# Float32 activations kept until the down stage, and 30 instead of 27 of 44 down groups by the seven-product scheme

## Chip, cores and metric

The kernel runs on one core of one Trainium2 chip. The metric is the device time of one execution in microseconds (us), the median of several runs. TensorE (PE in the profile) multiplies, VectorE (DVE) adds and subtracts elementwise, ScalarE (ACT) casts and copies, SyncE (SP) issues most loads, and GpSimd (POOL) issues some transfers.

## The reference, cut to what matters

One block of a network on 256 tokens of 2048 channels, in float32: three kinds of attention, gates, an output projection, and a feed-forward part with 5632 hidden channels.

```python
h = rms_norm(x, g_mix); proj = h @ w_in           # then three kinds of attention, gated
...
x = x + merged @ w_out
h2 = rms_norm(x, g_ffn)
u = causal_depthwise_conv(h2 @ w_up, conv_w, conv_b)
u_gate, u_val = jnp.split(u, 2, axis=-1)
x = x + (jax.nn.silu(u_gate) * u_val) @ w_down     # (256 x 5632) @ (5632 x 2048)
```

The change is in the last two products, here called the up stage (`h2 @ w_up`) and the down stage (`a @ w_down`, where `a` is the product of silu(u_gate) and u_val).

## The kernel before, in words

**Three passes for one float32 product.** TensorE multiplies a rounded float32 format (`fp32r`). A float32 operand is split into `hi` (its rounded value, cast by ACT) and `lo` (what is left, subtracted by DVE), and `three` issues three passes for one product: activation hi by weight hi (L382), activation lo by weight hi (L383), activation hi by weight lo (L384). The weights are split as they come (`parts`, L376 and L377): a tile of 128 x 1024 or 128 x 512 is cast into one of four `hi` tiles and subtracted into one of four `lo` tiles. A fifth part can only be cast when TensorE is done with the first one's `hi`, and subtracted when it is done with its `lo`. The raw weights land in a ring of six 512 KB tiles, loaded by SP; a tile comes free when its subtraction is done.

**The down stage.** It has two column blocks of 1024 (`nb` 0 and 1), each walked over 22 pairs of 128-channel rows of `w_down`. A pair is one of 44 groups in all, and a string in `d_plans` says in which order and in which way the groups go (`blocked`):

- `e` (`eight`): eight products, 24 passes of 512 columns; two parts of 1024, loaded plainly (1 MiB).
- `s` (`seven`): the same result by seven products, 21 passes; sums of weight blocks and sums of activation blocks take the place of one product. Four parts (three of 1024, one of 512). The sums of the weights were made in earlier stages and stored in a DRAM tile `kept`; what is loaded is 1.75 MiB. The seven products go into four `Y` banks and three of the four `X` banks of PSUM; after the block's last `s`, `gather` (L409 to L419) adds the `Y` banks to the result `xres`.
- `f` (`form`): the next pair's sums of activation blocks are made (`pair_sums`, L391 to L400: four DVE operations to sum, ACT casts, DVE subtractions).

Before, pairs 0 to 10 in block 0 and 0 to 15 in block 1 go by `s`: 27 of 44. The sums of the weights of two of them (pairs 14 and 15 of block 1) are made by GpSimd with transfers that accumulate in DRAM, late in the up stage (`sums_in_hbm`, `last_sums`). In the up stage each finished 128 x 256 product `a` is split at once (`split_to`, L175 cast and L176 subtract) into the tile `aT`; the last four of the 44 go to `a_ends`.

**Order.** The program text gives an order, and a scheduler of the framework then moves instructions on each engine's queue by its own estimates; only instructions marked `in_order` keep their place. Each engine works its queue strictly in that final order, and waits where an instruction's input isn't there. The end of the program is: the last two `e` groups, X banks added to `xres` on DVE (L1388, L1392), output stored by ACT's queue (L1390 to L1395).

The functions that the diff touches:

## Time and profile before

| what | us |
| --- | --- |
| median of 3 runs (1457.41 to 1457.68) | 1457.41 |
| the profiled execution, its device time | 1458.07 |
| its span from first to last instruction | 1456.4 |
| TensorE busy, of the span | 1451.0 (100%) |
| VectorE busy | 1229.0 (84%) |
| ScalarE busy | 857.1 (59%) |
| GpSimd busy | 31.8 (2%) |

The profile gives a start and a duration for each instruction, and for idle time of an engine what ended it. Successive passes of TensorE overlap, so the time that a pass costs is the distance between two starts, not its own duration. VectorE's instructions also overlap slightly. The down stage begins at 1230.9 us on TensorE.

### The profile page before, as it was taken

How to read it: one execution, taken by the hardware profiler on the slowest of the kernel's cores; microseconds unless marked ns; L12 is line 12 of the kernel's file. 1: busy time of each engine (PE TensorE's matmuls, PEld its weight loads, DVE VectorE, ACT ScalarE, POOL GpSimd, SP SyncE). 2: the span in 40 equal slices, each digit the busy share in tenths (PEclk: the TensorE clock that was granted, in tenths of full speed). 3: DMA queues.
4: the chain of work that ended last, by engine and by line, in shares of the span. 5: the costliest groups of instructions: out<-in, count | busy, mean ns of one | idle time of the engine just before them, and what ended most of it. 6: DMA issues, size and time to landing. Idle time of an engine off the chain costs nothing.

```text
span 1456.4 us, 20650 instructions
## 1 busy us (share of the span) xinstructions
PE 1451.0 (100%) x7290; PEld 1228.8 (84%) x7290; DVE 1229.0 (84%) x1824; ACT 857.1 (59%) x1222; POOL 31.8 (2%) x69
## 2 busy tenths in 40 slices
PE   9999999999999999999999999999999999999998
PEld 7888888888888888888888888888888888888887
DVE  5788778776898899998887888888888877999988
ACT  6755445464564555546676656556556566676775
POOL 0000011010000000000000000000000010000000
PEclk9999999999999999999999999999999999999999
DMA  8797899777668576788877888888888899789996
GB/s 288 223 355 252 308 341 327 267 246 220 213 205 267 181 227 199 270 262 264 303 218 233 289 271 303 281 271 300 282 280 296 275 258 258 247 286 340 326 338 233
DMA packets 169414, 393.41 MB, mean 270 GB/s; under 512 B 12906, under 2 KB 30206, under 8 KB 165086
## 3 DMA queue, kind: packets, MB, share of 16 engines
q1 hardware_dynamic: 165822, 384.87, 79.3%
q0 software_dynamic: 2160, 5.12, 2.0%
q10 hardware_dynamic: 1328, 2.11, 0.4%
q8 instruction: 57, 0.93, 0.3%
q14 instruction: 47, 0.39, 0.1%
HBM read 353.24 MB, written 43.00 MB: 272 GB/s over the span
## 4 chain that ended last, share of the span: by engine, by line
PE 100%; DVE 0%; issue 0%; DVEq 0%
PE u L1315 22%; PE u L1316 11%; PE xg L384 4%; PE xg L383 4%; PE xg L382 4%; PE xd L384 3%; PE xd L383 3%; PE xd L382 3%; PE s L384 2%; PE s L382 2%; PE f L382 2%; PE f L384 2%; PE s L383 2%; PE f L383 2%; PE b L384 2%; PE b L383 2%
## 5 line engine op out<-in xcount | busy, mean ns | idle before, releaser
L1315 PE MATMUL u<-hT,hi_u 128*128 128x512 f32 x1232 | 428.4, 394 | 0.0
L1316 PE MATMUL u<-hT,lo_u 128*128 128x256 f32 x1232 | 341.3, 277 | 0.0
L1315 PEld LDWEIGHTS u<-hT,hi_u 128*128 128x128 f32 x1232 | 231.0, 188 | 53.5
L142 DVE TENSOR_TENSOR lo_u<-raw_u,hi_u 128x1024 fp32r<-128x1024 f32 x176 | 215.1, 1222 | 72.2 <-ACT hi_u L141 71.7
L141 ACT CAST hi_u<-raw_u 128x1024 fp32r<-128x1024 f32 x176 | 184.7, 1050 | 133.3 <-PE u L1315 101.3
L1316 PEld LDWEIGHTS u<-hT,lo_u 128*128 128x128 f32 x1232 | 231.3, 188 | 0.0
L377 DVE TENSOR_TENSOR lo_d<-raw_d,hi_d 128x1024 fp32r<-128x1024 f32 x88 | 106.8, 1221 | 12.9 <-ACT hi_d L376 10.7
L376 ACT CAST hi_d<-raw_d 128x1024 fp32r<-128x1024 f32 x88 | 91.9, 1054 | 36.6 <-PE xd L383 12.6
L376 ACT CAST hi_g<-raw_g 128x1024 fp32r<-128x1024 f32 (+1 forms) x80 | 77.1, 972 | 47.6 <-PE xg L383 21.3
L377 DVE TENSOR_TENSOR lo_g<-raw_g,hi_g 128x1024 fp32r<-128x1024 f32 (+1 forms) x80 | 88.7, 1119 | 5.7 <-ACT hi_g L376 5.3
L384 PE MATMUL xg<-lo_g,xT 128*128 128x512 f32 x175 | 68.1, 389 | 0.0
L382 PE MATMUL xg<-hi_g,xT 128*128 128x512 f32 x175 | 68.1, 389 | 0.0
L383 PE MATMUL xg<-hi_g,xT 128*128 128x512 f32 x175 | 68.1, 389 | 0.0
L141 ACT CAST hi_f<-raw_f 128x1024 fp32r<-128x1024 f32 (+1 forms) x40 | 38.6, 967 | 47.1 <-PE f L383 27.5
L1315 PE MATMUL u<-hT_rest,hi_u 128*128 128x512 f32 x176 | 62.0, 394 | 0.0
L141 ACT CAST hi_b<-raw_b 128x1024 fp32r<-128x1024 f32 x32 | 33.7, 1052 | 45.8 <-PE b L383 14.5
L142 DVE TENSOR_TENSOR lo_f<-raw_f,hi_f 128x1024 fp32r<-128x1024 f32 (+1 forms) x40 | 44.4, 1117 | 17.9 <-ACT hi_f L141 17.8
L1265 ACT ACTIVATE y<-u,taps 128x256 f32<-128x256 f32 x88 | 49.5, 595 | 16.8 <-DVE u L1260 16.7
L141 ACT CAST hi_s<-raw_s 128x1024 fp32r<-128x1024 f32 (+1 forms) x40 | 38.2, 961 | 35.7 <-PE s L383 18.8
L142 DVE TENSOR_TENSOR lo_s<-raw_s,hi_s 128x1024 fp32r<-128x1024 f32 (+1 forms) x40 | 44.6, 1123 | 17.1 <-ACT hi_s L141 17.1
L376 ACT CAST hi_t_g<-t_g 128x1024 fp32r<-128x1024 f32 x30 | 31.5, 1051 | 41.4 <-PE xg L383 39.7
L376 ACT CAST hi_t_d<-raw_t_d 128x1024 fp32r<-128x1024 f32 (+1 forms) x54 | 43.5, 836 | 18.9 <-PE xd L383 11.7
(554 smaller groups left out, 3548.8 us busy)
## 6 DMA issues: line engine op xcount, KB each, us to landing
raw_u<-in_w_up_dram SPq DMA_DIRECT2D x176, 512.0 KB, 4.9
raw_g<-in_w_in_dram SPq DMA_DIRECT2D x96, 512.0 KB, 4.5
raw_d<-in_w_down_dram SPq DMA_DIRECT2D x61, 512.0 KB, 5.8
pre_d<-in_w_down_dram SPq DMA_DIRECT2D x17, 1024.0 KB, 7.6
kept_d<-pre_d SPq DMA_DIRECT2D x17, 1024.0 KB, 6.9
raw_f<-in_w_in_dram SPq DMA_DIRECT2D x32, 512.0 KB, 5.7
raw_s<-in_w_in_dram SPq DMA_DIRECT2D x32, 512.0 KB, 5.7
raw_t_d<-kept_d SPq DMA_DIRECT2D x27, 512.0 KB, 6.1
```

Source lines behind the costliest of these rows:

```text
L141: pin(nc.scalar.copy(hi[:, :m], raw[:, :m]))
L142: pin(nc.vector.tensor_tensor(lo[:, :m], raw[:, :m], hi[:, :m].bitcast(F32), ALU.subtract))
L376: nc.scalar.copy(hi[:, :n], src)
L377: nc.vector.tensor_tensor(lo[:, :n], src, hi[:, :n].bitcast(F32), ALU.subtract)
L382: fix(nc.tensor.matmul(o, lhsT=ah, rhs=w[0], start=first, stop=False))
L383: fix(nc.tensor.matmul(o, lhsT=al, rhs=w[0], start=False, stop=False))
L384: fix(nc.tensor.matmul(o, lhsT=ah, rhs=w[1], start=False, stop=last))
L1265: nc.scalar.activation(y, u[:, 2:], AF.Identity, scale=tap(2), bias=tap(3))
L1315: nc.tensor.matmul(ps[i], lhsT=hi[:, j, c], rhs=hT(k + j), start=first, stop=False)
L1316: nc.tensor.matmul(ps[i][:, :S], lhsT=lo[:, j, c], rhs=hT(k + j)[:, :S], start=False, stop=last)
```

## The change

**Groups.** The plans are new. `t` is a `seven` whose weight sums are not loaded: its two plain tiles are loaded, and four DVE additions of 128 x 512 make the sums (`made`). Block 0 has 8 `e` and 14 sevens (two of them `t`: pairs 4 and 9); block 1 has 6 `e` and 16 sevens (three `t`: pairs 6, 10 and 13), in the order of pairs 5 to 15, then 0 to 4. The GpSimd sums are gone. 25 groups have their weight sums made ahead, in both versions.

**Activations.** For pairs 0 to 13 the up stage writes the float32 product and the three block sums into one tile `a_raw` of eight 128 x 128 blocks (`raw_sums`), and splits nothing. In the down stage an `f` of block 0 splits seven of these blocks at once (`split_raw`: one ACT cast and one DVE subtraction of 128 x 896); `lo` goes where the previous pair's raw tile was, `hi` into one of nine slots. Pairs 9 to 13 overwrite the slots of 0 to 4, so `hi` of 0 to 4 is stored to DRAM (448 KB each, ACT's queue) and loaded again in block 1 (`back`, SP's queue). Only pairs 14 and 15 still have `pair_sums` in the down stage.

```diff
-        "efefefef" + "sef" * 4 + "ssefsfssfssee",
-        "efsss" * 3 + "efssfsssssee",
+        "efefeffef" + "sfsfsfs" + "eftfss" + "fsfs" + "etfsfs" + "ss" + "ee",
+        "estse" + "fsfste" + "fssfte" + "fsfsfss" + "sss" + "ee",
...
+        def made(p):
+            raw0, raw1 = load(2 * p), load(2 * p + 1)
+            raw2 = raw_tile(f"raw_t_{name}{nb}_{p}")
+            raw3 = t4_tile(f"raw_t4_{name}{nb}_{p}")
+            nc.vector.tensor_tensor(raw2[:, :512], raw0[:, :512], raw0[:, 512:], ALU.add)
+            nc.vector.tensor_tensor(raw0[:, 512:], raw0[:, 512:], raw1[:, 512:], ALU.add)
+            nc.vector.tensor_tensor(raw2[:, 512:], raw2[:, :512], raw1[:, 512:], ALU.add)
+            nc.vector.tensor_tensor(raw3, raw2[:, 512:], raw1[:, :512], ALU.add)
+            return raw0, raw1, raw2, raw3
...
+    def raw_sums(p):
+        v = raw_blocks(p).rearrange("p (i q) -> p i q", i=8)
+        a01 = v[:, 7:8].to_broadcast([P, 2, P])
+        nc.vector.tensor_tensor(v[:, 2:4], v[:, 5:7], a01, ALU.subtract)
+        nc.vector.scalar_tensor_tensor(v[:, 0], v[:, 2], -1.0, v[:, 6], ALU.mult, ALU.subtract)
+        nc.vector.tensor_tensor(v[:, 1], v[:, 0], v[:, 4], ALU.add)
...
+            if p < n_raw:
+                c = 768 - 256 * j
+                nc.vector.tensor_tensor(raw_blocks(p)[:, c : c + S], g, y, ALU.mult)
+                if j:
+                    raw_sums(p)
+                return
             nc.vector.tensor_tensor(g, g, y, ALU.mult)
-            a_done.append(a_pair(f // 2)[:, f % 2])
-            split_to(a_done[-1], g)
+            split_to(a_pair(p)[:, j], g)
...
+    def split_raw(p):
...
+        hi = place_at(p % n_at)
+        place_of[p] = hi, lo
+        nc.scalar.copy(hi, w[:, : 7 * P])
+        nc.vector.tensor_tensor(lo, w[:, : 7 * P], hi.bitcast(F32), ALU.subtract)
+        if p < moved:
+            left[p] = dram.tile([P, 7 * P], F32, tag=f"left_{p}", name=f"left_{p}")
+            nc.scalar.dma_start(left[p], hi.bitcast(F32))
+
+    def back(p):
+        hi = place_at((moved + p) % n_at)
+        place_of[p] = hi, place_of[p][1]
+        nc.sync.dma_start(hi.bitcast(F32), left[p])
```

In the up stage and before it, TensorE's order is the same in both. In the down stage the order moves, and three places of it matter below. The rows give the line, the operation, and output and inputs by the program's names; line 360 of the changed kernel is line 377 of the one before (subtract into `lo`), and 365, 366 and 367 are 382, 383 and 384 (the three passes).

First, VectorE ahead of the first weight part of pair 4 of block 0 (tiles `d0_8`, `d0_9`), which is the first `t`. Before, the subtractions of parts stand among the sums for the activations (`fw`):

```order
L391 TENSOR_TENSOR fw_7_12345<-aT_6752 128x512
L377 TENSOR_TENSOR lo_d0_36_12312<-raw_d0_36_12309,hi_d0_36_12311 128x1024
L394 TENSOR_TENSOR fw_7_12345<-fw_7_12345 128x256
L377 TENSOR_TENSOR lo_d0_37_12330<-raw_d0_37_12327,hi_d0_37_12329 128x1024
L395 SCALAR_TENSOR_TENSOR fw_7_12345<-fw_7_12345 128x128
L400 TENSOR_TENSOR aT_6752<-fw_7_12345,aT_6752 128x128
L396 TENSOR_TENSOR fw_7_12345<-fw_7_12345 128x128
L377 TENSOR_TENSOR lo_d0_8_12364<-raw_d0_8_12354,hi_d0_8_12363 128x1024
L400 TENSOR_TENSOR sf_11752<-fw_7_12345,sf_11752 128x3x128
L377 TENSOR_TENSOR lo_d0_9_12374<-raw_d0_9_12357,hi_d0_9_12373 128x1024
```

VectorE at the same place of the changed kernel, where line 1375 is the split of a pair's activations and lines 463 to 466 are the four additions of the `t`:

```order
L360 TENSOR_TENSOR lo_d0_36_12153<-raw_d0_36_12150,hi_d0_36_12152 128x1024
L360 TENSOR_TENSOR lo_d0_37_12171<-raw_d0_37_12168,hi_d0_37_12170 128x1024
L1375 TENSOR_TENSOR a_lo8_12186<-a_raw8_9060,sf_more_12187 128x896
L463 TENSOR_TENSOR raw_t_d0_4_12194<-raw_d0_8_12190 128x512
L1375 TENSOR_TENSOR a_lo9_12237<-a_raw9_9104,sf_11730 128x896
L464 TENSOR_TENSOR raw_d0_8_12190<-raw_d0_8_12190,raw_d0_9_12192 128x512
L465 TENSOR_TENSOR raw_t_d0_4_12194<-raw_t_d0_4_12194,raw_d0_9_12192 128x512
L1375 TENSOR_TENSOR a_lo10_12332<-a_raw10_9514,sf_11730 128x896
L466 TENSOR_TENSOR raw_t4_d0_4_12195<-raw_t_d0_4_12194,raw_d0_9_12192 128x512
L360 TENSOR_TENSOR lo_d0_8_12201<-raw_d0_8_12190,hi_d0_8_12200 128x1024
```

Three splits and four additions now stand between the subtraction of the preceding `e` group (`d0_37`) and that of the `t` group's first part.

Second, TensorE at that group. Before, a part's three passes follow each other, with its `lo` third:

```order
L382 MATMUL yd0_0_11986<-hi_d0_8_12363,aT_6752 128x512
L383 MATMUL yd0_0_11986<-hi_d0_8_12363,aT_6752 128x512
L384 MATMUL yd0_0_11986<-lo_d0_8_12364,aT_6752 128x512
L382 MATMUL yd0_3_11989<-hi_d0_8_12363,sf_11752 128x512
L383 MATMUL yd0_3_11989<-hi_d0_8_12363,sf_11752 128x512
L384 MATMUL yd0_3_11989<-lo_d0_8_12364,sf_11752 128x512
```

TensorE in the changed kernel, same group:

```order
L365 MATMUL yd0_0_11953<-hi_d0_8_12200,sf_11730 128x512
L366 MATMUL yd0_0_11953<-hi_d0_8_12200,a_lo4_11948 128x512
L365 MATMUL yd0_3_11956<-hi_d0_8_12200,sf_11730 128x512
L366 MATMUL yd0_3_11956<-hi_d0_8_12200,a_lo4_11948 128x512
L365 MATMUL xd0_0_0_11731<-hi_d0_9_12210,sf_11730 128x512
L366 MATMUL xd0_0_0_11731<-hi_d0_9_12210,a_lo4_11948 128x512
L365 MATMUL xd0_0_1_11732<-hi_d0_9_12210,sf_11730 128x512
L366 MATMUL xd0_0_1_11732<-hi_d0_9_12210,a_lo4_11948 128x512
L365 MATMUL yd0_2_11955<-hi_t_d0_4_12220,sf_11730 128x512
L366 MATMUL yd0_2_11955<-hi_t_d0_4_12220,a_lo4_11948 128x512
L367 MATMUL yd0_0_11953<-lo_d0_8_12201,sf_11730 128x512
L367 MATMUL yd0_3_11956<-lo_d0_8_12201,sf_11730 128x512
```

The first pass that needs `lo` of `d0_8` is now the eleventh of its group and no longer the third. At some other places of the changed down stage the `lo` passes are put back in the same way, by a few passes.

Third, VectorE at the end of the program. Before, the last addition of `gather` (L419) stands behind the first of the four X additions (L1388):

```order
L413 TENSOR_TENSOR xres_again_5681<-xres_again_5681,e_1024_13834 128x512
L415 TENSOR_TENSOR e_1024_13834<-e_1024_13834,yd1_3_12895 128x512
L416 TENSOR_TENSOR xres_again_5681<-xres_again_5681,e_1024_13834 128x512
L418 TENSOR_TENSOR e_1024_13834<-e_1024_13834,yd1_2_12894 128x512
L1388 TENSOR_TENSOR xres_again_5681<-xres_again_5681,xd1_0_0_12839 128x512
L419 TENSOR_TENSOR xres_again_5681<-xres_again_5681,e_1024_13834 128x512
L1388 TENSOR_TENSOR xres_again_5681<-xres_again_5681,xd1_0_1_12840 128x512
L1388 TENSOR_TENSOR xres_again_5681<-xres_again_5681,xd1_1_0_12841 128x512
L1388 TENSOR_TENSOR xres_again_5681<-xres_again_5681,xd1_1_1_12842 128x512
L1392 TENSOR_TENSOR xres_again_5681<-xres_again_5681,apart_13870 128x256
```

VectorE at the end of the changed kernel:

```order
L396 TENSOR_TENSOR xres_again_5681<-xres_again_5681,e_1024_13749 128x512
L398 TENSOR_TENSOR e_1024_13749<-e_1024_13749,yd1_3_12836 128x512
L1432 TENSOR_TENSOR xres_again_5681<-xres_again_5681,xd1_0_0_12793 128x512
L399 TENSOR_TENSOR xres_again_5681<-xres_again_5681,e_1024_13749 128x512
L1432 TENSOR_TENSOR xres_again_5681<-xres_again_5681,xd1_0_1_12794 128x512
L401 TENSOR_TENSOR e_1024_13749<-e_1024_13749,yd1_2_12835 128x512
L1432 TENSOR_TENSOR xres_again_5681<-xres_again_5681,xd1_1_0_12795 128x512
L402 TENSOR_TENSOR xres_again_5681<-xres_again_5681,e_1024_13749 128x512
L1432 TENSOR_TENSOR xres_again_5681<-xres_again_5681,xd1_1_1_12796 128x512
L1436 TENSOR_TENSOR xres_again_5681<-xres_again_5681,apart_13785 128x256
```

The four late additions of `gather` (L398 to L402) are now spread among the X additions (L1432), and the last of them stands between the third and the fourth. Just ahead of the last two `e` groups, in both blocks, the addition of the second Y bank (L393, L410 before) also moved: before, it stood behind the subtractions of the first two parts of the `ee`; now it stands ahead of them.

More of the change, by code (lines that the diff above doesn't have):

```diff
@@ L236, in hybrid_block @@
     by_k = lambda w: w[0].rearrange("(k p) n -> p k n", p=P)
-    o_sevens = (0, 1, 2, 3, 6)
-    pairs = lambda name, n: o_sevens if name == "o" else range(n)
+    pairs = lambda name, nb, n: sevens.get((name, nb), range(n))
     sums_of = {}
@@ L243, in hybrid_block @@
         for name, w, plans in (("o", w_out, o_plans), ("d", w_down, d_plans))
-        for nb, plan in enumerate(plans)
-        for pr in pairs(name, plan.count("s"))
-        if (name, nb, pr) not in in_hbm
+        for nb in range(len(plans))
+        for pr in sevens[name, nb]
+        if (name, nb, pr) not in here
         for h in range(2)
@@ L464, in eight, with brought @@
                                 three(apart[0], *a_of(p, j, t), wj, j == 0, j == 1)
-        def seven(p, first, last):
+        def brought(p):
             kept = sums_of[name, nb, p]
@@ new lines, in hybrid_block, with form, f_of, raw_parts @@
+    steps = deque([split_raw, p] for p in range(n_raw))
+    steps.extend([form_sums, p] for p in range(n_raw, n_pairs))
+    steps.extend([back, p] for p in range(moved))
+    def form():
+        f, p = steps.popleft()
+        f(p)
+    def f_of(p, f):
+        if p < n_raw:
+            return raw_parts(p, f)
+        if f == FS1:
+            return a_of(p, 0, 1)
+        return [sums_at(p)[:, f, i] for i in range(2)]
+    def raw_parts(p, which):
+        i = AT[which]
+        hi, lo = place_of[p]
+        return [v[:, i * P : (i + 1) * P] for v in (hi, lo)]
```

132 lines of the change are left out of this document (61 added, 71 removed).

## The prediction

> **What bounds the kernel now.** I read the page first (busy shares, clock, chain), then the down stage in stretches, then single rows of TensorE and VectorE there, the waits, and the loads.
>
> ```profile
> span 1456.4 us, 20650 instructions
> ...
> PE 1451.0 (100%) x7290; PEld 1228.8 (84%) x7290; DVE 1229.0 (84%) x1824; ACT 857.1 (59%) x1222; POOL 31.8 (2%) x69
> ...
> PEclk9999999999999999999999999999999999999999
> ...
> PE 100%; DVE 0%; issue 0%; DVEq 0%
> ```
>
> The chain that ended last is TensorE from end to end, at full granted clock throughout. So a pass less is worth its distance, and anything else costs only where it makes TensorE wait. The next question is how near the other engines are in the down stage. Columns: stretch, length, then busy us (x instructions) of PE, PEld, DVE, ACT, POOL, clock, DMA share, GB/s.
>
> ```profile
> 1230.90:1332.00 101.10, 101.10 (x448) 83.65 (x447) 96.92 (x154) 70.90 (x98) 0.00 (x0) 1.00 0.87 291
> 1332.00:1451.00 119.00, 119.00 (x528) 98.50 (x527) 108.93 (x141) 78.49 (x99) 0.00 (x0) 1.00 0.88 307
> 1430.00:1440.00 10.00, 10.00 (x46) 8.29 (x45) 9.25 (x10) 8.33 (x10) 0.00 (x0) 1.00 0.93 372
> 750.00:1230.00 480.00, 480.00 (x2774) 419.88 (x2773) 399.18 (x653) 286.19 (x440) 12.89 (x20) 1.00 0.85 274
> ```
>
> In block 0 (first row) VectorE is busy 96.92 of 101.10 us: nearly a second bound. ScalarE has room everywhere, and the up stage (last row) has 80 us free on VectorE.
>
> **The passes.** Two successive rows of TensorE, and the program's last one:
>
> ```profile
> 1318.41 0.39 PE L384 MATMUL yd<-lo_d,aT 128*128 128x512 f32 x1
> 1318.64 0.39 PE L382 MATMUL yd<-hi_d,sf 128*128 128x512 f32 x1
> ...
> 1321.13 0.39 PE L384 MATMUL yd<-lo_t_d,aT 128*128 128x512 f32 x1
> ...
> 1452.03 0.28 PE L384 MATMUL apart<-lo_d,a_ends 128*128 128x256 f32 x1
> ```
>
> From 1318.41 to 1321.13 are 12 passes: 2.72 us, 0.2265 each. Three pairs, all in block 0, go from 24 to 21 passes: 9 fewer, 9 x 0.2265 = **-2.04 us**. The rest of TensorE's work is the same, so this is also the most that can be gained.
>
> **VectorE's work.** Its prices:
>
> ```profile
> L377 DVE TENSOR_TENSOR lo_d<-raw_d,hi_d 128x1024 fp32r<-128x1024 f32 x88 | 106.8, 1221 | 12.9 <-ACT hi_d L376 10.7
> L377 DVE TENSOR_TENSOR lo_t_d<-raw_t_d,hi_t_d 128x512 fp32r<-128x512 f32 x27 | 18.5, 686 | 0.9 <-ACT hi_t_d L376 0.9
> L494 DVE TENSOR_TENSOR t_g<-raw_g 128x512 f32<-128x512 f32 x15 | 10.3, 684 | 0.0
> L391 DVE TENSOR_TENSOR fw<-aT 128x512 f32<-128x512 f32 x16 | 11.0, 688 | 0.3
> L394 DVE TENSOR_TENSOR fw<-fw 128x256 f32<-128x256 f32 x16 | 6.7, 420 | 0.1
> L395 DVE SCALAR_TENSOR_TENSOR fw<-fw 128x128 f32<-128x128 f32 x16 | 4.6, 287 | 0.2
> L396 DVE TENSOR_TENSOR fw<-fw 128x128 f32<-128x128 f32 x16 | 4.6, 285 | 0.1
> L400 DVE TENSOR_TENSOR aT<-fw,aT 128x128 fp32r<-128x128 f32 x31 | 8.3, 284 | 0.0
> L400 DVE TENSOR_TENSOR sf<-fw,sf 128x384 fp32r<-128x384 f32 x9 | 5.0, 552 | 0.4 <-ACT sf L398 0.4
> L176 DVE TENSOR_TENSOR aT<-y,aT 128x256 fp32r<-128x256 f32 x40 | 16.0, 419 | 0.5 <-ACT aT L175 0.5
> ```
>
> One forming of sums before: 0.69 + 0.42 + 0.29 + 0.29 + 0.28 + 0.55 = 2.5 us. A split of 128 x 896, which no row shows, lies between the 512 and the 1024 subtraction (0.69 and 1.22); in proportion 1.09. The sums of one `t`: 4 x 0.684 = 2.74. A pair from `e` to `s`: parts 3 x 1.22 + 0.69 for 2 x 1.22, +1.9. Block 0: -11 x 2.5 + 14 x 1.09 + 2 x 2.74 + 3 x 1.9 = -1.1, so 95.8 busy of 99.1 us: as full as before. Block 1: -5 x 2.5 + 2 x 2.5 + 3 x 2.74 = +0.7 of 119. On the average nothing is gained or lost; it depends on places.
>
> In the up stage a pair's two subtractions (2 x 0.42) give way to three operations (0.42, 0.29, 0.29): +0.16 us for each of 14 pairs, 2.2 us against 80 free, and ScalarE loses two casts a pair. Cost 0, unless TensorE should be caught within 0.2 us of a part, which no wait there shows. The GpSimd sums that go were off the chain: 0.
>
> **How much lead a part has.** The ring of four sets it.
>
> ```profile
> 1318.34 1.83 DVE L377 TENSOR_TENSOR lo_t_d<-raw_t_d,hi_t_d 128x1024 fp32r<-128x1024 f32 x2
> ...
> ACT hi_d L376 <- PE xd L383: 12.6, 24, 1.7
> ```
>
> The first of these two subtractions ends at 1318.34 + 1.22 = 1319.56; its first pass is the row at 1321.13 above: 1.57 us of lead in a run of sevens. ScalarE's casts wait 24 times for TensorE to free a tile, so the lead cannot pile up.
>
> **First `t` (block 0, pair 4).** VectorE at the stage's start:
>
> ```profile
> 1241.26 1.22 DVE L377 TENSOR_TENSOR lo_d<-raw_d,hi_d 128x1024 fp32r<-128x1024 f32 x1
> 1242.40 0.42 DVE L176 TENSOR_TENSOR a_ends<-y,a_ends 128x256 fp32r<-128x256 f32 x1
> 1242.73 0.48 DVE L1267 SCALAR_TENSOR_TENSOR y<-u,taps,y 128x256 f32<-128x256 f32 x1
> 1243.13 1.22 DVE L377 TENSOR_TENSOR lo_d<-raw_d,hi_d 128x1024 fp32r<-128x1024 f32 x1
> 1244.27 0.42 DVE L1273 TENSOR_TENSOR y<-y,y 128x256 f32<-128x256 f32 x1
> ```
>
> Operations start 0.085 us before the one ahead ends (1242.40 against 1242.48), so 1024 columns take 1.135, 512 take 0.60, 256 take 0.335, and a split 1.00. The last product (row at 1244.27) has two subtractions of 1024 fewer in front of it in the new order, so it starts between 1242.0 and 1244.3. From there to the end of `d0_8`'s subtraction stand, itself with it, 17 subtractions of 1024, 11 splits, 4 subtractions of 512, 4 additions, and one of 256: 19.3 + 11 + 2.4 + 2.4 + 0.3 = 35.4 us, after the product's own 0.335. That ends between 1277.8 and 1280.1; ring waits like those above add up to 1.5 us to the early end. TensorE's first pass with this `lo` has 5 x 24 + 4 x 21 + 10 = 214 passes ahead of it: 1230.9 + 214 x 0.2265 = 1279.4. In the old order (the third pass of the group) it would be 1277.6. So the passes that were put back cover what the additions cost: **+0.2**, ends 0 and 0.9.
>
> [...]
>
> **The other four `t`.** Their additions stand in stretches with more room (block 1), with 2.4 us of additions ahead of parts whose `lo` is put back 5 or 3 passes: +0.3 together, ends 0 and 1.0.
>
> **`gather` ahead of the last `ee`.** The addition of bank Y1 waits for the last pass into it, and the subtraction of `d0_40` (`d1_40`) is now queued behind it. From that pass's start: 0.39 for the pass, 0.12 to be seen, 0.60, 1.22, 0.12 = 2.45 us; TensorE has 9 other passes between, so needs it after 10 x 0.2265 = 2.27. Late 0.2 in each block, and bank Y0's copy on ScalarE ahead of the cast of `t_d0_13` another 0.1: **+0.5**, ends 0 and 1.8 (two subtractions 0.6 later each).
>
> **Tail.**
>
> ```profile
> 1448.20 0.69 DVE L1388 TENSOR_TENSOR xres_again<-xres_again,xd 128x512 f32<-128x512 f32 x1 [0.44 <-PE xd L384]
> 1448.81 0.69 DVE L419 TENSOR_TENSOR xres_again<-xres_again,e 128x512 f32<-128x512 f32 x1
> ...
> 1450.92 1.40 DVE L1388 TENSOR_TENSOR xres_again<-xres_again,xd 128x512 f32<-128x512 f32 x2 [0.67 <-PE xd L384]
> 1452.43 0.42 DVE L1392 TENSOR_TENSOR xres_again<-xres_again,apart 128x256 f32<-128x256 f32 x1
> 1452.36 0.34 ACTq L1390 DMA_DIRECT2D out_dram<-xres_again  x1
> 1452.88 0.34 ACTq L1393 DMA_DIRECT2D out_dram<-xres_again  x1
> ```
>
> After TensorE's last pass (1452.03 + 0.28) VectorE needs one addition. From 1450.92 on it had two additions and then 0.1 us to spare; L419 with 0.60 to 0.69 now stands between these two: **+0.55**, ends 0.2 and 0.7.
>
> **Transfers.**
>
> ```profile
> raw_d<-in_w_down_dram SPq DMA_DIRECT2D x61, 512.0 KB, 5.8
> raw_t_d<-kept_d SPq DMA_DIRECT2D x27, 512.0 KB, 6.1
> ```
>
> A seven loads 1.835 MB in 4.76 us, 385 GB/s, a `t` 1.05 MB. Five stores of 448 KB leave ScalarE's queue near 1245 us, at the 0.34 us of issue that the output rows show, where ScalarE has 30% free; the five `back` loads replace no critical load, and the slots they wait for were read last one or more groups earlier. 0, with +1.5 as upper end (below).
>
> **Sum.** -2.04 + 0.2 + 0.3 + 0.5 + 0.55 = -0.5. The profiled execution of 1458.07 us (span 1456.4) becomes 1457.6, and the median 1457.41, which lies 0.66 under it, becomes **1456.9 us**. Without any new wait but the tail it is 1455.9. 0.2% is 2.9 us, about what can be told from no change: 1454.5 and 1460.3.
>
> **Rivals.**
>
> *All new waits are hidden.* -2.04 and a tail of 0 to 0.55: 1455.4 to 1455.9. For it: every lateness above is below 0.3 us and comes from estimates. Against: VectorE is as full as before, with more places where it stands near.
>
> *Slower: a `t`'s additions wait for their load.* VectorE works in order, so an addition that waits holds the splits and subtractions behind it. The second tile of pair 4 takes the slot of `d0_6`, whose subtraction ends 11.7 us of queued work before that of `d0_8` (1279 in the middle), at 1267.3; loaded in 5.8 us it lands at 1273.1, and the addition that reads it comes 3.9 us before the same end, at 1275.1: 2.0 us to spare; by the same count only 0.7 at pair 13 of block 1. A landing of L us costs each of five groups L - 5.8 less that margin (1.3 in the mean). At 8.5 us that is 5 x 1.4 = 7: 1463.3. It is slower by over 0.2% from about 7.9 us. Against it: a median of 5.8 in stretches that move more bytes than a `t` does.
>
> *Transfers bind in the last run.* Seven sevens and two `back` loads move 13.8 MB in 33.3 us, 413 GB/s, where the row of 1430 to 1440 shows 372 and the rate needed there was 385. If 385 were the top, 35.8 us: 2.5 longer, less 1.0 of lead (two groups of 4.76, less 6.1 for landing and 2.4 for splitting): +1.5, 1458.4. [...]
>
> **How the numbers follow.** Small waits as summed (1455.9 to 1458.3): 0.62. All hidden: 0.18. Additions that wait for loads: 0.10. Transfers: 0.10. The range reaches from all hidden, 1455.4, over the likeliest's upper end and the transfers at 385 to 1459.5, which leaves out most of the load case and the worst of the transfers. Faster by over 0.2% needs more than the passes give: 0.03. Slower, half of the load case and a third of the transfers and a rest: 0.11. Same: 0.86.
>
> **What would show it.** TensorE's down stage with 972 passes and 0.5 to 1.5 us of idle time, at `lo_d0_8`, `lo_t_d0_13`, `lo_d0_40` and `lo_d1_40`; VectorE busy about 95.8 in block 0; the last addition some 0.6 us after the last pass rather than 0.1. The prediction is wrong if TensorE idles in the up stage, if a VectorE addition waits for a load, if a cast waits for a load in the last run, or if 128 x 896 takes more than 1.1 us.

## Result: slower by 8 us, and the profile after

| | before | after |
| --- | --- | --- |
| median (range) of 4 runs beside each other, us | 1457.55 (1457.41 to 1459.03) | 1465.78 (1463.42 to 1466.71) |
| profiled execution, us | 1458.07 | 1466.71 |
| its span, us | 1456.4 | 1465.0 |
| down stage, from TensorE's first pass to the start of its last, us | 221.14 | 228.91 |

The ratio is 1.0052, with an interval of 1.0034 to 1.0069: slower by more than 0.2%, where 1456.9 us and no change were forecast. The time lies above the range's end of 1459.5.

The page of the changed kernel, the lines that answer to those shown of before (busy us, share of the span and instructions; then the chain that ended last):

```profile
span 1465.0 us, 20537 instructions
...
PE 1454.1 (99%) x7281; PEld 1225.0 (84%) x7281; DVE 1229.8 (84%) x1781; ACT 848.4 (58%) x1173; POOL 20.1 (1%) x51
...
PE 93%; DMA 3%; DVE 2%; issue 1%; ACT 0%; SPq 0%; DVEq 0%; ACTq 0%
```

TensorE has its 9 passes fewer (7281 for 7290), but the chain no longer runs on TensorE alone: DMA and VectorE have entered it. The down stage in two stretches (columns as in the same view of before):

```profile
1231.60:1332.00 100.40, 99.99 (x438) 81.10 (x437) 96.06 (x112) 75.57 (x93) 0.00 (x0) 1.00 0.88 311
1332.00:1460.50 128.50, 124.38 (x536) 98.26 (x536) 109.84 (x127) 74.62 (x84) 0.00 (x0) 1.00 0.83 290
```

Block 0 is nearly dense, with VectorE at 96.06 of 100.40. The time was lost in block 1: 124.38 busy of 128.50, and even the busy part has passes spread by short waits. No engine is full there and the granted clock is 1.00; the DMA share is lower than in block 0. The waits of the changed kernel from 1231 to 1464 us (who waits, for whom: us in total, times, longest):

```profile
ACT hi_t_d L359 <- DMA raw_t_d<-kept_d: 14.2, 12, 6.1
...
ACT hi_d L359 <- DMA raw_d<-kept_d: 8.0, 9, 3.5
ACT hi_d L359 <- DVE raw_d L464: 7.4, 2, 4.5
...
ACT hi_d L359 <- DMA raw_d<-in_w_down_dram: 6.6, 15, 1.2
...
DVE raw_t_d L463 <- DMA raw_d<-in_w_down_dram: 1.6, 1, 1.6
```

Before, ScalarE's casts waited above all for TensorE to free a `hi` tile (12.6 us in 24 waits, 11.7 in 12 and 9.1 in 21, the three longest rows of the same view), which means that they were ahead of it. Now they wait above all for loads and for L464, the `t`'s addition into its first tile.

TensorE's starts that come later than 0.2265 us after the one ahead, summed by place: first `t` 0.54, the groups of pairs 6 and 7 behind it 0.56, two `ee` 0.11 each, start of block 1 1.55, groups of pairs 8 and 9 (1371 to 1376 us) 1.79, end of pair 9 and `t` of pair 10 2.35 (1.6 of it at the `t`), end of pair 12 and `t` of pair 13 1.77 (1.15 at the `t`), another 0.11: 8.9 us. With -2.04 for the passes and 0.9 in smaller bits this is the 7.77 by which the down stage grew.

**Start of block 1.** Single rows of the changed kernel (VectorE, SP's queue, ScalarE, TensorE):

```profile
1343.29 0.69 DVE L402 TENSOR_TENSOR xres_again<-xres_again,e 128x512 f32<-128x512 f32 x1
...
1344.00 0.38 SPq L454 DMA_DIRECT2D raw_t_d<-kept_d  x1
...
1350.69 1.57 ACT L359 CAST hi_t_d<-raw_t_d 128x1024 fp32r<-128x1024 f32 x2 [6.06 <-DMA raw_t_d<-kept_d]
...
1353.06 0.50 PE L367 MATMUL yd<-lo_t_d,sf 128*128 128x512 f32 x1 [0.53 <-DVE lo_t_d L360]
```

L402 is the last addition of block 0's `gather`. Its input `e` now stands in a slot of the ring of six load tiles (`gather(n0, Y, raw_d)`), so SP cannot issue the load that takes this slot until L402 has ended at 1343.98; it issues at 1344.00, the data are there at 1350.69, 6.06 us after ScalarE was ready, and TensorE is late.

**`t` of pair 10.** Its additions and what follows:

```profile
1381.44 0.68 DVE L463 TENSOR_TENSOR raw_t_d<-raw_d 128x512 f32<-128x512 f32 x1
1382.16 0.69 DVE L464 TENSOR_TENSOR raw_d<-raw_d,raw_d 128x512 f32<-128x512 f32 x1
1382.48 0.40 PE L367 MATMUL xd<-lo_t_d,sf 128*128 128x512 f32 x1
1383.02 2.00 ACT L359 CAST hi_d<-raw_d 128x1024 fp32r<-128x1024 f32 x2 [2.83 <-PE xd L367]
1384.12 0.50 PE L365 MATMUL yd<-hi_d,sf 128*128 128x512 f32 x1 [1.24 <-ACT hi_d L359]
```

The view names TensorE as the releaser of the cast, but the row of L464 ends at 1382.85 and the cast starts 0.17 later: it waited for the addition, the addition stood behind the previous group's subtractions in VectorE's queue, and TensorE's first pass of the group waits for the cast. (L367 reads a `lo` tile, so it frees no `hi`.) At pair 13 it is the same: a cast there waited 3.92 us, put down to TensorE, and started 0.17 us after L464 had ended at 1403.98. So a cast waited for L464 at four of the five `t`, and not only at the two that the view names.

**Tail.** The last addition of the program:

```profile
1460.50 0.28 PE L367 MATMUL apart<-lo_d,a_ends 128*128 128x256 f32 x1
...
1461.58 0.42 DVE L1436 TENSOR_TENSOR xres_again<-xres_again,apart 128x256 f32<-128x256 f32 x1
```

It starts 1.08 us after the start of the last pass, before 0.40: +0.68. From that start to the end of the span it is 4.50 against 4.33, since what follows the addition, the output's transfer above all, was shorter (3.42 against 3.93 us); why it was isn't shown.

### The profile page after: what moved, and what is told of

The parts are those of the page before. It is cut to its first block, busy times and chain, and to the rows that moved or that the text cites. A ratio compares the mean times of both kernels' runs of the same rounds, so it can differ in the third digit from the quotient of the medians.

```text
span 1465.0 us, 20537 instructions
## 1 busy us (share of the span) xinstructions
PE 1454.1 (99%) x7281; PEld 1225.0 (84%) x7281; DVE 1229.8 (84%) x1781; ACT 848.4 (58%) x1173; POOL 20.1 (1%) x51
## 4 chain that ended last, share of the span: by engine, by line
PE 93%; DMA 3%; DVE 2%; issue 1%; ACT 0%; SPq 0%; DVEq 0%; ACTq 0%
PE u L1331 22%; PE u L1332 11%; PE xg L365 4%; PE xg L366 4%; PE xg L367 4%; PE s L365 2%; PE s L367 2%; PE f L365 2%; PE f L367 2%; PE s L366 2%; PE f L366 2%; PE b L365 2%; PE b L367 2%; PE b L366 2%; PE xd L367 2%; PE xd L365 2%
## 5 line engine op out<-in xcount | busy, mean ns | idle before, releaser
L367 PE MATMUL xg<-lo_g,xT 128*128 128x512 f32 x175 | 68.1, 389 | 0.0
L360 DVE TENSOR_TENSOR lo_t_d<-raw_t_d,hi_t_d 128x1024 fp32r<-128x1024 f32 (+1 forms) x60 | 54.8, 953 | 8.3 <-ACT hi_t_d L359 7.8
L359 ACT CAST hi_t_d<-raw_t_d 128x1024 fp32r<-128x1024 f32 (+1 forms) x60 | 47.6, 834 | 19.0 <-DMA raw_t_d<-kept_d 14.2
L1275 ACT ACTIVATE y<-u,taps 128x256 f32<-128x256 f32 x88 | 48.9, 595 | 13.8 <-DVE u L1270 13.6
```

What stands on the lines that cost most here:

```text
L359: nc.scalar.copy(hi[:, :n], src)
L360: nc.vector.tensor_tensor(lo[:, :n], src, hi[:, :n].bitcast(F32), ALU.subtract)
L367: fix(nc.tensor.matmul(o, lhsT=ah, rhs=w[1], start=False, stop=last))
L1275: nc.scalar.activation(y, u[:, 2:], AF.Identity, scale=tap(2), bias=tap(3))
```

## Experiments

Three suspects came out of the traces: the work tile of `gather` in the ring of load tiles; the additions made on the spot; and the five loads of `hi` (`back`). The rivals among them were whether the additions cost by VectorE's time, by their own slot of the ring, by waiting for loads, or by the wait of the cast behind them; and whether the reloads cost by SP's queue or by their bytes. Ratios are to the kernel before, run on the same chip beside each (1457.8 to 1458.4 us); the kernels below ran on five chips. By the intervals of two ratios, the difference between two of these kernels is known to some 2 us to either side.

**The tile of `gather` out of the ring.**

```diff
+    spare = lambda name: ff.tile([P, PIECE], F32, tag=f"raw{n_raw - 1}", bufs=1, name=name)
-            lambda n0, Y: gather(n0, Y, raw_d), None, form, apart,
+            lambda n0, Y: gather(n0, Y, spare), None, form, apart,
```

> Only the gather's 4 KB work tile is moved out of the ring of six load tiles, into the tile that pair 13's float32 activations have left. Theory A (loads are issued late because tiles and waits that are not loads stand in their way: the gather's tile and the sums' tiles in the ring, and the reloads of activations in SyncE's queue): the idle time of TensorE at the start of block 1 (1.5 us between 1352 and 1358 in the changed kernel's profile) goes, 1.0 to 1.6 us faster than the changed kernel (about 1464.3). Theory B (the additions on the spot make VectorE late): no change there, 0 to 0.3. Theory C (the transfers' bandwidth is the bound): the load goes out earlier but lands no earlier, 0 to 0.3.

Measured 1462.73 us (1461.77 to 1463.59); 1.0032 (1.0020 to 1.0044): 3.05 less than the changed kernel. The idle time at 1352 to 1357 us is gone, and the last addition starts 0.40 us after the start of the last pass again. In the profiled executions the down stage is 2.97 us shorter (225.94) and what follows it 0.50. This is one of the causes: the start of block 1 is late by 1.3 us in a kernel below that keeps this tile in the ring and has the reloads on another queue, and not late at all in three others that contain this edit. What is left shows in the waits of this kernel's down stage:

```profile
ACT hi_d L359 <- DVE raw_d L464: 13.6, 5, 3.6
```

Five waits, one for each `t`. The kernels below that say "on top" contain this edit, and are compared with 1462.73.

**The reloads from another queue, and everything else out of the ring.** Two kernels: the changed one with `back` issued by GpSimd; and one on top with the two remaining `fw` tiles out of the ring as well and `back` issued by ScalarE.

```diff
-        nc.sync.dma_start(hi.bitcast(F32), left[p])
+        nc.gpsimd.dma_start(hi.bitcast(F32), left[p])     # the second kernel: nc.scalar
...
-        pair_sums(a_pair(p), raw_d(f"fw_{p}"), ...)
+        pair_sums(a_pair(p), spare(f"fw_{p}"), ...)       # the second kernel
```

> Only the five reloads of activations are issued from GpSimd's queue and not from SyncE's, with the same bytes. Theory A: weight loads no longer stand behind a reload that waits for TensorE; the idle time at 1371 to 1376 (1.9 us) goes and a part of that at 1381 to 1386 (2.2 us): 1.5 to 3 us faster than the changed kernel. Theory B: 0. Theory C: the same bytes at nearly the same time, 0 to 0.5.

> Gather's tile and the two sums' tiles out of the ring, and the reloads on ScalarE's queue. Theory A: idle time left only at the groups with additions on the spot, 4 to 6 us faster than the changed kernel (1460 to 1462). Theory B: 0 to 1 us faster. Theory C: 0 to 1 us faster.

Measured 1466.2 (1.0055, 1.0042 to 1.0068; one run of six took 3768.55) and 1462.44 (1.0034, 1.0022 to 1.0046). The first is no better than the changed kernel, the second no better than the `gather` edit alone. Where the reloads are issued isn't a cause, nor are the `fw` tiles.

**All sums made ahead.** No `t`; the five groups' sums are made in the up stage, on a denser schedule than before.

```diff
-    here = {
+    here = set() and {
-        pair_sums_ahead(..., 8, 1, 5, delay=DU)
+        pair_sums_ahead(..., 6, 1, 5, delay=DU)   # the second kernel: 6, 2, 4, on top
```

> The weight sums of the five groups that were summed on the spot are made ahead in the up stage as for the other 25 (every 6 steps and not every 8), so that all 30 load them; tiles and queues as in the changed kernel. Theory B: the idle time at the five groups goes (first one 0.5, those of 1381 to 1386 and 1401 to 1407 4.0 together), 3 to 5 us faster, 1461 to 1463. Theory A: idle time at 1352 and 1371 stays, and what follows it is about the same, since the queue's delays are carried on: 0 to 2 faster. Theory C: each of the five now loads 1.75 and not 1 MiB: 0 to 3 us slower.

> All 30 weight sums ahead, with the up stage's steps spaced so that its loads are there when VectorE comes to them (every 6 steps, added after 2, stored after 4), and gather's tile out of the ring as in e1. Theory B2 (a group summed on the spot needs a longer turn of the ring of six load tiles: load, two additions, cast, subtraction, some 11 us against the 9.5 us that two groups take; one with its sums loaded needs no more than 9.5): the down stage is as dense as before the change, 219.5 to 221 us from first to last pass where e1 has 225.9, and the time is 1456 to 1459 if the up stage stays whole. Rival (the reloads and the split of activations cost it): down stage still above 223.

Measured 1474.38 (1.0107, 1.0094 to 1.0120) and 1469.58 (1.0075, 1.0062 to 1.0087). The down stage without `t` and without that tile is dense:

```profile
1241.80:1462.30 220.50, 220.31 (x973) 180.99 (x972) 196.44 (x219) 151.99 (x175) 0.00 (x0) 1.00 0.90 329
```

220.5 us with all five reloads still there. But it starts at 1241.8: the up stage took 501.5 us, where it takes 489.95 both before and after the change. TensorE waited there for `lo` of the up weights (5.4 us in 5 waits), VectorE for the loads of its additions (5.7 us in 5 waits), and the casts for the loads of the up weights (74.5 us in 39 waits, before 15.3 in 8); which of these delays sets the time wasn't told apart. Making the sums ahead moves the price to the up stage and raises it.

**Order and slots of a `t`.** On top: the part of the second tile, which needs no addition, multiplied first; and, in another kernel, block 1's sum tiles out of the ring.

```diff
+            if (name, nb, p) in here:
+                of_raw1()          # parts(raw1) and its two products, ahead of raw0's
...
-            raw2 = raw_tile(f"raw_t_{name}{nb}_{p}")
+            raw2 = (spares[0] if nb else raw_tile)(f"raw_t_{name}{nb}_{p}")
```

> As e1, and in the groups summed on the spot the part that needs no sum (the second tile) is cast and multiplied first, so that the additions have one more part's time. Theory B2: the wait of the first cast on the second addition goes (1.4 at 1380, 0.4 at the first such group), the ring's turn for the first tile is as long as before: 1 to 3 us faster than e1 (1462.7). Rival (VectorE simply has too much to do there): the same work, 0 to 0.5.

> As e1, and in block 1 the tile that takes two of the sums made on the spot is no tile of the ring, so that the loads behind it go out one tile earlier. Theory B2: 1 to 3 us faster than e1. Rival (bandwidth): loads go out earlier and land no earlier, 0 to 0.5. Rival (VectorE has too much to do): 0.

Measured 1463.48 (1.0033, 1.0023 to 1.0043) and 1462.71 (1.0032, 1.0021 to 1.0044): no gain from either. With the other part first, the casts waited for loads instead (13.6 us in 18 waits for `raw_d<-in_w_down_dram`).

**The kernel before with one load tile fewer.** Its down stage with a ring of five.

```diff
-    raw_d = lambda name: raw_tile(name, lambda name: place([P, PIECE], F32, "raw", name))
+    def raw_d(name):
+        loads[0] += 1
+        if loads[0] <= 10 or loads[0] % (WBUFS + 1) < WBUFS:
+            return wp.tile([P, PIECE], F32, tag="raw", name=name)
+        return place([P, PIECE], F32, "raw", name)
```

> The kernel before the change with five load tiles instead of six in the down stage. If two groups' time (9.5 us) is just what a turn of the ring of six needs, a ring of five (1.67 groups, 7.9 us) makes each group in a run of sevens wait: 27 sevens, 15 to 40 us slower. If loads have room to spare in the kernel before, 0 to 3 us slower.

Measured 1462.91 (1.0035, 1.0022 to 1.0047), +4.5 us, far less than was expected if the ring stood exactly at its limit. One slot in steady use is worth about 4.5 us here, so a few turns of a slot lost to `gather` can cost two or three.

**Reloads left out.** On top, without the five loads (the products of pairs 0 to 4 in block 1 then use other activations).

```diff
-        nc.sync.dma_start(hi.bitcast(F32), left[p])
```

> As e1, but the five reloads of activations in block 1 (2.3 MB) are left out; the passes read what the slots hold. Theory C2 (the reloads come in bursts with weight loads, those land in 7 to 9 us and not 6, and the groups summed on the spot, which need their tiles earlier, are what suffers): 2 to 4 us faster than e1 (1462.7), the idle time at 1368 to 1382 gone. Theory B3 (the additions are too much for VectorE at their places, whatever the loads do): 0 to 1 us faster.

Measured 1460.65 (1458.79 to 1462.12, 11 runs; 1.0016, 1.0008 to 1.0025): 2.1 us less, about as much as the uncertainty of the difference. The idle time of the groups of pairs 8 and 9 is gone in the profile, and the wait for L464 stays (12.0 us in 4).

**Additions left out, and additions of other data.** On top: no additions, the parts of the sums cast from the second tile; and the same with as many additions of the same size, on other data and with unused results.

```diff
-            nc.vector.tensor_tensor(raw2[:, :512], raw0[:, :512], raw0[:, 512:], ALU.add)
... 
-            return raw0, raw1, raw2, raw3
+            return raw0, raw1, raw1, raw1[:, :512]
...
+            for _ in range(4):     # the second kernel
+                nc.vector.tensor_tensor(raw3, other, other, ALU.add)
```

> As e1, but the twenty additions on the spot are left out, with the same loads, casts, subtractions and passes; the parts that would hold sums are cast from the second tile, and the sums' ring tile is not taken. Theory B3: the down stage is as dense as with all sums ahead (220.5 us), 4 to 5.5 us faster than e1. Theory C2: 0 to 2 us faster, since the loads come as before.

> As e10 (the additions' results are not used, parts cast from the second tile), but twenty additions of 128 x 512 stand at the places of the old ones, on other data that is there long before. VectorE has the same work, and no cast or addition waits for another. If VectorE's time at these places is the price: about e1's time, 1461.5 to 1463. If the price is that an addition waits for its load and a cast for the addition: e10's time, 1457.3 to 1458.5.

Measured 1457.84 (1456.22 to 1459.25; 0.9999, 0.9990 to 1.0007) and 1456.88 (1455.60 to 1458.02; 0.9993, 0.9984 to 1.0001), 11 runs each. Without additions 4.9 us less; with the same VectorE work but nobody waiting for it, no more than that. The second kernel in two stretches:

```profile
1230.10:1332.00 101.90, 101.90 (x452) 84.40 (x451) 99.54 (x117) 78.89 (x95) 0.00 (x0) 1.00 0.92 321
1332.00:1450.00 118.00, 117.67 (x524) 97.06 (x522) 107.03 (x123) 73.34 (x81) 0.00 (x0) 1.00 0.85 304
```

In block 0 VectorE is busy 99.54 of 101.90 us, and TensorE has no gap; in block 1, with three of the `t`, TensorE is idle for 0.33 us. So VectorE has the time for the additions, and the price goes when nothing waits for them. The expectation was that they stay at their places, and they did not: with nothing tied to them the scheduler put the four of pair 10 about 10 us earlier (137.7 us into the down stage, 147.4 with the `gather` edit alone), and at the first `t` two of the three splits behind the first subtraction. What part this new order has in the gain wasn't told apart.

**Which dependence.** Three kernels. With no additions but one of 128 x 32 that needs both loads ahead of the first cast; on top with the real additions' outputs but other data as inputs; and on top with only L464 left out, so that the first tile goes unsummed.

```diff
+            nc.vector.tensor_tensor(raw0[:, 512:544], raw0[:, 512:544], raw1[:, 512:544], ALU.add)
...
+            nc.vector.tensor_tensor(raw2[:, :512], other, other, ALU.add)     # and so on, raw0 unsummed
...
-            nc.vector.tensor_tensor(raw0[:, 512:], raw0[:, 512:], raw1[:, 512:], ALU.add)
```

> As e10, but one addition of 128 x 32 per group, 0.1 to 0.2 us, that needs both loads and ahead of which the first tile is not cast. VectorE has hardly any work from it, and the wait for the loads is there. If VectorE's time is the price: 1457.5 to 1459. If the wait for loads is: 1460 to 1463.

> As e1, with the four additions of each of the five groups, their ring tile and the casts that wait for them, but the additions read other data that is there long before, and the first tile is cast without an addition. If the price is that additions (and the cast behind them) wait for late loads: 1457 to 1459. If it is the ring tile that sums take, or the casts of the sums waiting for VectorE: 1460.5 to 1463.

> As e1, but of the four additions the one into the first tile is left out, so that its cast waits only for its load, while the other three wait for both loads and VectorE's queue with them. If the price is that the first cast comes after two additions: 1457.5 to 1459.5. If it is the additions that wait for loads and hold VectorE's queue, or the sums' ring tile: 1461 to 1463.

Measured, 11 runs each: 1457.92 (1.0001, 0.9992 to 1.0009), 1459.32 (1.0010, 1.0001 to 1.0019), 1460.58 (1.0017, 1.0009 to 1.0026). Without the large additions, a first cast that waits for both loads and for a 128 x 32 addition costs nothing, though the casts do wait for it:

```profile
ACT hi_d L359 <- DVE raw_d L461: 6.3, 4, 2.6
```

Here all three splits at the first `t` stand ahead of the first subtraction, as with the `gather` edit alone, and at pair 13 the small addition waited 1.40 us for its load. So neither VectorE's work alone nor the handover alone showed a price; the price comes where a cast waits for additions that take their time. Leaving out L464 alone gives back 2.15 of the 4.9; additions of other data, with the first tile unsummed, give back 3.4; the first of these is about as large as its uncertainty. In the kernel without L464 the casts of the sums wait in its place:

```profile
ACT hi_t_d L359 <- DVE raw_t_d L464: 5.7, 2, 3.6
```

(L464 is there the addition into `raw_t_d`.) So the wait goes to the next part whose cast needs an addition. The last 1.5 us, between 1459.32 and 1457.84, may be the casts of the sums behind their additions or the sum tile's slot of the ring, or no difference at all: the two intervals overlap. The slot alone, freed in block 1, gave nothing.

**All three left out.** No additions, no reloads, `gather`'s tile outside.

```diff
-            return raw0, raw1, raw2, raw3
+            return raw0, raw1, raw1, raw1[:, :512]
...
-        nc.sync.dma_start(hi.bitcast(F32), left[p])
```

> Gather's tile out of the ring, no reloads, no additions. If these three are all that the change costs beyond what was forecast: the time of the forecast without waits and with its tail, 1455.5 to 1456.5. If they overlap, or something else costs, 1456.5 to 1457.8.

Measured 1457.81 (1456.16 to 1460.42, 11 runs; 0.9999, 0.9991 to 1.0008), the same as with the reloads. So the reloads cost 2.1 us beside the additions and nothing that shows without them: as far as the intervals tell, the two prices don't add up.

**Additions on GpSimd.** On top, all four additions of `made` moved.

```diff
-            nc.vector.tensor_tensor(raw2[:, :512], raw0[:, :512], raw0[:, 512:], ALU.add)
+            nc.gpsimd.tensor_tensor(raw2[:, :512], raw0[:, :512], raw0[:, 512:], ALU.add)
...
```

> As e1, with the twenty additions on GpSimd, which has nothing else to do in the down stage, and not on VectorE. Theory B3: VectorE is relieved of 2.7 us a group; if GpSimd adds 128 x 512 in up to about 1.5 us, 2 to 5 us faster than e1; where it takes more, or holds up VectorE, slower. Theory C2: slower by what GpSimd takes longer, 0 to 5 us.

Measured 1467.85 (1.0066, 1.0054 to 1.0078), 5.1 more. One group of the additions (columns of the groups: count, busy us, mean ns, idle before):

```profile
L466 POOL TENSOR_TENSOR raw_t_d<-raw_t_d,raw_d 128x512 f32<-128x512 f32 x5 | 10.8, 2158 | 0.4
```

An addition of this group takes 2.16 us, where the same line takes 0.69 on VectorE, and the time rose though VectorE is relieved. That the cast behind an addition waits longer here, the chain again and not the engine's share, is argued from these numbers: the waits of these casts aren't shown.

**Fewer `t`, and `t` at other places.** On top: three `t` (27 sums made ahead); and block 1's `t` each directly behind an `e`, whose groups are longer.

```diff
-    }
+    } - {("d", 0, 4), ("d", 1, 10)}     # and delay=6 for the sums ahead
...
-        "estse" + "fsfste" + "fssfte" + "fsfsfss" + "sss" + "ee",
+        "etsse" + "ftsfse" + "ftssfe" + "fsfsfss" + "sss" + "ee",
```

> As e1, but of the five groups summed on the spot two (pair 4 of block 0, pair 10 of block 1) get their sums ahead: 27 made ahead in the up stage at its old spacing, from its sixth step on. If each such group has its own price (e1 shows TensorE idle for 1.2 at the first and 2.2 at pair 10 with what follows them), 2 to 4 us faster than e1, 1459 to 1461, when the up stage stays whole; if the price comes from all of them together (the stage's ledger), 2/5 of 5.4, 2.2 us; if it is the reloads, 0 to 1.

> As e1, with the same number of additions, but in block 1 each group summed on the spot follows a group by eight (pairs 5, 8 and 11) and does not end a run of sevens (pairs 6, 10 and 13). If the price is that it comes where a run of sevens has used up the lead: the idle time of 1375 to 1403 in e1 mostly goes, 2 to 4 us faster than e1 (1458.7 to 1460.7). If it is the total work or bytes: the same as e1 within 1.

Measured 1468.5 (1461.89 to 1473.12; 1.0071, 1.0048 to 1.0093) and 1468.07 (1.0075, 1.0061 to 1.0089). Neither gain came. In the first, the six runs lie in two clumps (1461.89 to 1464.97, and 1472.03 to 1473.12), and the profiled execution, of the lower clump, shows the up stage 2.45 us longer by the two sums more. Its down stage, 225.00 us, is only 0.9 shorter than that of the `gather` edit's kernel: the sums of pair 10 are loaded there, and TensorE still starts 2.6 us late at the end of pair 10 and in the group behind it, where casts wait for loads (1.76 us for `raw_t_d<-kept_d`). So not all of the lateness at a `t` goes with the `t`. In the second, one wait hides everything else. SP's queue and TensorE:

```profile
1368.04 0.38 SPq L1383 DMA_DIRECT2D sf<-left  x1
1373.72 0.32 SPq L456 DMA_DIRECT2D raw_t_d<-kept_d  x1
...
1376.37 0.42 SPq L450 DMA_DIRECT2D raw_d<-in_w_down_dram  x1
```

```profile
1379.08 0.39 PE L367 MATMUL xd<-lo_t_d,sf 128*128 128x512 f32 x1
1386.82 0.80 PE L365 MATMUL yd<-hi_d,sf 128*128 128x512 f32 x1 [7.35 <-ACT hi_d L359]
```

SP's next load waits until 1373.72 for its slot (5.2 us, for a subtraction into `lo_t_d`), the first tile of pair 10, an `s` here, is queued behind it and is issued at 1376.37, and TensorE does nothing from 1379.5 to 1386.8. In this kernel, where a load stands in SP's order decided more than which group is a `t`.

## Why the prediction was wrong, point by point

- **Passes, -2.04.** Right: 9 passes fewer on the page, and with few gaps left the down stage takes 220.5 us with all the work in it (sums made ahead) and 219.74 with the detached additions; less the late starts in them, 1.28 and 0.71, both are within 0.2 of 221.14 - 2.04 = 219.10.
- **Up stage, GpSimd sums, 0.** Right: 489.95 us from the first up pass to the first down pass in both.
- **VectorE's work.** Right: 96.06 us busy in block 0 for 95.8, and a split of 128 x 896 took 1.09 as estimated.
- **First `t`, +0.2 (0 to 0.9).** Measured 0.54, inside the ends, but by another step. The working was done for the eleventh pass, the first that needs `lo`; what came late is the first pass of the group, which needs `hi`. Its cast at 1277.18 had waited 2.94 us for L464. The 0.56 in the groups of pairs 6 and 7, where casts wait for loads, was not in the working; whether it follows from this `t` isn't shown.
- **"The other four `t`", +0.3 together (0 to 1.0).** The step that failed. At the `t` of pairs 10 and 13 with the ends of the groups ahead TensorE starts 4.1 us late, and all additions together cost 4.9 with the `gather` edit in. They were priced by VectorE's time and by passes put back, stretch by stretch. The runs showed that this time is free where nothing waits for it (20 detached additions cost nothing), and the rows show the round in which it is not: TensorE frees a `hi` tile (at pair 10 of the changed kernel, a load lands), the last cast and subtraction of the group ahead go, then VectorE gets to the additions, then ScalarE casts the sum, and only then TensorE has its first `hi` of the group. The prediction put back only the `lo` passes; a `t`'s first pass needs `hi`, which waits for an addition, and ScalarE's later casts are queued behind it. This was no step of the working at all.
- **The ring.** "The slots they wait for were read last one or more groups earlier" was said of the reloads; that `gather`'s tile, and with it L402, becomes such a slot stands in the diff and was priced nowhere. 3.05 us.
- **Transfers, 0 (to +1.5).** The upper end was looked for in the last run, where it wasn't: the 35 us from 1410 move 375 GB/s with TensorE busy throughout (35.00 us). That transfers cost more than these 1.5 us, which the range ("the worst of the transfers") and the chance of slower ("a third of the transfers") count with, no run shows: what the runs showed in its place is this stretch without a gap. In the last run, from 1410 to 1446 us, casts did wait for loads (7.3 us in 15 waits), which the prediction had named as a sign of being wrong, but at no price. The five reloads cost 2.1 us, in the middle of block 1 and only beside the additions. Loads there, from issue to landing (after, 1340 to 1410 us, two rows; then before, 1332 to 1400):

```profile
raw_t_d<-kept_d SPq DMA_DIRECT2D x7, 512.0 KB, 7.6
raw_d<-kept_d SPq DMA_DIRECT2D x7, 256.0 KB, 7.6
```

```profile
raw_t_d<-kept_d SPq DMA_DIRECT2D x10, 512.0 KB, 6.4
raw_d<-kept_d SPq DMA_DIRECT2D x11, 256.0 KB, 6.9
```

The same loads take up to 1.2 us longer, though the stretch moves fewer bytes per us than the dense one behind it (293 and 297 GB/s, then 375): they are issued in bunches, when a wait of SP ends. That the bunches are what makes them longer is argued and not shown; without the additions, `raw_t_d<-kept_d` took 7.9 us there and cost nothing.
- **`gather` ahead of `ee`, +0.5.** 0.11 in each block: inside the ends, half the size. The 0.12 "to be seen" from a pass's end to VectorE is 0.04 in a row of before (the pass 1450.49 + 0.39, the addition at 1450.92).
- **Tail, +0.55.** 0.68 at the last addition; 0.17 in the span.
- **The rival "a `t`'s additions wait for their load"** (0.10; 1463.3) is nearest to what came: its count of 0.7 us to spare at pair 13 was rightly the weakest, and an addition does wait there (SP's rows of its two tiles, then VectorE's):

```profile
1391.63 1.47 SPq L419 DMA_DIRECT2D raw_d<-in_w_down_dram  x2
...
1399.82 0.69 DVE L463 TENSOR_TENSOR raw_t_d<-raw_d 128x512 f32<-128x512 f32 x1 [1.56 <-DMA raw_d<-in_w_down_dram]
```

The first tile was issued at 1391.63 and let L463 go at 1399.82, some 8 us later: the condition of that rival, "from about 7.9 us", was met at this `t`. It was given little because a median of 5.8 was taken for a load's time. But it is one of five: at pair 10 the additions waited for VectorE, not for a load, and in the `gather` edit's kernel the five waits are for L464. And the small addition that waited 1.40 us for the same load cost nothing. (The rival's own sum is a little off: 7 us on 1456.9 is 1463.9, or 1463.4 where they replace the 0.5 of the `t`.)

By sum: 1457.55 - 2.04 + 3.05 (`gather`'s tile, with the tail) + 4.9 (additions, and by way of them the reloads' 2.1) = 1463.5, where 1465.78 was measured. The other 2.3 us are in the kernel with all three left out as well (1457.81, where the passes alone give 1455.5). Half a microsecond of them is the kernel before, which took 1458.02 beside that one; 1.8 remain, known to 1.3 to either side. That kernel's profiled execution has 0.8 of lateness in its down stage (219.90 for 219.10), but it was the fastest of the eleven, 1456.16. What makes up the rest stays open.

No version was found that beats both kernels: the best one that does the whole work is the `gather` edit with everything out of the way, 1462.44, still slower than before (1.0022 to 1.0046).

## What to carry to other kernels

An operation put between a load and the cast that feeds the bounding engine is priced by what it adds to that chain, not by the room that its engine has: the same work cost nothing here when nobody waited for it (1456.88 us with the detached additions), and a wait for a short operation cost nothing either (1457.92 with one addition of 128 x 32). Ask what the cast's engine has to wait for, what is queued behind that cast, and where the group's first pass stands, before asking whether the engine has time. Whatever takes a tile from a ring of load buffers, a work tile above all, is priced as a load that cannot be issued until that tile's last reader is done (here 1344.00, after L402 at 1343.98; the price was 3.05 us). In these runs a busy share, even 98% (99.54 of 101.90 us), was no price, and neither was a median time to landing; what to work out is the lead of the earliest-needed part of each group.

## What the runs showed of the hardware

- TensorE's clock after a long wait. In the kernel with `t` at other places, three stretches around the 7.3 us without work:

```profile
1380.00:1387.00 7.00, 0.18 (x1) 0.18 (x2) 0.74 (x2) 1.17 (x2) 0.00 (x0) 0.82 0.96 311
1387.00:1392.00 5.00, 4.96 (x13) 3.43 (x14) 5.00 (x5) 3.48 (x5) 0.00 (x0) 0.56 0.62 209
1392.00:1400.00 8.00, 8.00 (x37) 6.61 (x36) 6.95 (x9) 4.45 (x5) 0.00 (x0) 1.00 0.82 268
```

  The granted clock (the column behind POOL's) was 0.82, then 0.56 for 5 us in which 13 passes went where 22 fit at 0.2265: some 2 us more. In narrower stretches it is 1.00 from 1379.50 to 1384.50, with no pass at work, 0.50 from 1384.60 to 1391.30, and 1.00 from 1391.40 on: here it was halved some 5 us after the last pass had ended, and given back some 4.5 us after the first pass behind the wait had started at 1386.82. In the changed kernel it is 1.00 from 1231.6 to 1464.2 us, the longest distance between two starts of passes there being 1.64 us (1382.48 to 1384.12), and 0.50 from 1464.3 to 1464.9, where the last pass had started at 1460.50.
- GpSimd's float32 addition of 128 x 512 took 2.16 us in the group shown, VectorE's 0.684 in the row of L494 before and 0.69 in the same line (L466) of the changed kernel.
- VectorE was 97.7% busy over block 0 (99.54 of 101.90 us, detached additions) beside a TensorE without gaps, and one load tile of six was worth only 4.5 us (1462.91, ring of five).
